# Column sums of two norms and a LayerNorm as pairs of fp32r products with a constant tile

## The chip, the cores and the metric

One core of a Trainium2 chip. The metric is device time in microseconds (us) of one execution; lower is better. PE is TensorE (matmuls; PEld its weight load), DVE is VectorE, ACT ScalarE, POOL GpSimd, SP SyncE, which issues most DMAs. Line numbers with L are those of the kernel before, unless the changed program is named.

## The reference, cut to what matters

One layer of a decoder trunk on 256 prompt rows and 8 × 4 sample rows, all of 2048 channels, in fp32:

```python
h = rmsnorm(x, norm1_g)                                   # x * rsqrt(mean(x^2) + EPS) * g
proj = h @ w_in + b_in                                    # 2048 -> 3072: a, gate, z
u = a * sigmoid(gate)
c = silu(layernorm(depthwise_causal_conv(u_ext, conv_w, conv_b), ln_g, ln_b))
d = multiscale_pool(z_ext, pos0)
p = einsum("btgc,gce->btge", d, pool_w) * pool_scale
x = x + concat([c, p]) @ w_out                            # 2048 -> 2048
h2 = rmsnorm(x, norm2_g)
x = x + square(relu(h2 @ w_ff1)) @ w_ff2                  # 2048 -> 8192 -> 2048
y = rmsnorm(x, norm_f)
```

The outputs are y and the last inputs of the convolution and of the pooling (states).

## The kernel before

**Layout.** All activations are transposed: channels on the 128 partitions, the T = 288 rows of x as columns. xT holds x as 16 tiles of 128 channels. [...]

**Products.** Every large product is done in fp32r with both factors split into a high and a low part, as three matmuls per 128 × 128 weight tile and 288 columns: high·high, low weight·high, high·low activation. Each is one row of L313 in the profile. There are 8,112 of them. `gemm` (L298) makes a group: two banks (256 output channels) times 8 or 16 tiles k of the input. The order of the tiles' parts within a pair of k is fixed; `classes`, a string of 0 and 1, overrides it for the first products of a group (by the parity of tile plus part), and TURN is one such string. `between` names places in a group at which another piece of work is put; the products that follow are issued after its last matmul.

**Weights.** They come by DMA as fp32 (wr, 6 buffers), ACT copies them to fp32r (whi, L263), and the low part (wlo) is made by DVE (L268), POOL (L271) or ACT with a DMA that adds (L265). whi and wlo have 5 buffers each, so each cast on ACT waits until PE is done with a tile five back; which one that is shows in the program's semaphores.

**Stages**, in PE's order: w_in (24 column blocks; conv groups c0 to c7, pool groups p0 to p3 and their own small products P0 to P3), then w_out in two halves of eight groups of 48 products each: first the pool half (input mixp), then, behind LayerNorm and SiLU, the conv half (input mixc). Both halves are added to xT (L554, L575). Then ff1 and ff2 in four chunks, and the final norm.

**The sums.** For a norm `rsqrt_sums` (L219) computes with the squares as weights and a column of ones as moving data: three matmuls (six records, fp32 in two passes each, L228) give the sums as 96 partitions × 3 columns. On these 96 × 3 numbers Sqrt, reciprocal and one correction step run (L234 to L241), and `spread` (L244) multiplies them, broadcast, with the identity (L248, six records) so that each of 128 partitions has the row of 288 factors. The LayerNorm's mean is a product of a matrix of ones with sum_c and with the last c (L525, L526), fp32 in two passes. The placement: the first norm's sums in the first gemm at k = 15 and its rows in the third at k = 2; the LayerNorm by

```python
    BETWEEN = {5: {4: ln_mean}, 6: {6: ln_sums}, 7: {2: ln_rows}}
```

that is, mean in group 5 of the pool half, sums in group 6, rows in group 7. `load_table` (L204) loads ACT's table for the function that comes next. `ln_sums` subtracts the mean from the four c tiles (L531), squares them on ACT (L533), adds on DVE (L537, L538). The rows multiply c into n (L559), SiLU (L562) and a split into mx high (L564) and low (L565) give mixc.

**What sets the order.** Each engine runs its instructions in program order; a scheduler with a simulated timeline makes that order at build time from the code's order, priorities (`later` lowers one) and `issue_after`. So an instruction that waits holds up all that stands behind it on its engine.

## Time and profile before

| | us |
|---|---|
| median of 3 runs | 1090.91 (1090.12 to 1091.37) |
| profiled execution | 1087.89 |
| its span | 1086.1 |
| PE busy | 1071.3 (99%) |
| DVE busy | 632.8 (58%) |
| ACT busy | 476.1 (44%) |
| POOL busy | 181.5 (17%) |
| DMA | 190.71 MB, mean 176 GB/s |

A row of a timeline reads: start, length, engine, line, operation, out<-in, shapes, xcount and, in brackets, the engine's idle time before it and what ended it. A run of like instructions is one row. A matmul's length in a timeline contains its latency (0.29 for one of 288 columns), so successive rows overlap; the pace is seen from start to start. The chain of waits follows the work back from the last instruction; its pieces are listed by start and length.

### The profile page before, as it was taken

The page shows a single profiled execution, that of the slowest core. Times are in us where ns is not written, and L with a number is a line of the kernel's source. Part 1 is how long each engine was busy: PE and PEld are TensorE (multiplying, and loading weights), DVE is VectorE, ACT ScalarE, POOL GpSimd, SP SyncE. Part 2 cuts the span into 40 slices and gives each one's busy share as a digit, 9 for nine tenths or more (in the row PEclk, how much of TensorE's full clock was granted, in tenths as well). Part 3 has the DMA queues.
Part 4 walks back from the last instruction along what each step waited for, and adds up shares of the span by engine and source line. Part 5 has one row for each costly group of instructions (what it writes and reads, how often), then busy time and mean ns, then how long its engine had stood idle before and what let it go on. Part 6 is the DMA issues. An engine that isn't in the chain of part 4 may idle for free.

```text
span 1086.1 us, 19607 instructions
## 1 busy us (share of the span) xinstructions
PE 1071.3 (99%) x8206; PEld 1069.0 (98%) x8206; DVE 632.8 (58%) x812; ACT 476.1 (44%) x584; POOL 181.5 (17%) x212
## 2 busy tenths in 40 slices
PE   8999999999999999999999999999999999999996
PEld 8999999999999999999999999999999999999996
DVE  7899999678555444445454444545544445554553
ACT  8655445475544433334443333444433334444441
POOL 0889989613000000000000000000000000000000
PEclk9999999999999999999999999999999999999998
DMA  9896468545555555555555555555555555555522
GB/s 328 275 278 180 136 174 251 182 152 179 159 171 169 165 171 173 166 167 174 167 167 172 172 164 170 172 169 167 173 168 164 173 173 165 169 172 167 168 76 88
DMA packets 58120, 190.71 MB, mean 176 GB/s; under 512 B 6192, under 2 KB 11312, under 8 KB 58032
## 3 DMA queue, kind: packets, MB, share of 16 engines
q1 hardware_dynamic: 56752, 185.53, 54.4%
q0 software_dynamic: 1008, 3.67, 1.9%
q8 instruction: 64, 1.05, 0.4%
q10 hardware_dynamic: 272, 0.26, 0.1%
q14 instruction: 24, 0.20, 0.0%
HBM read 185.16 MB, written 4.28 MB: 174 GB/s over the span
## 4 chain that ended last, share of the span: by engine, by line
PE 96%; ACT 1%; DVE 1%; issue 1%; DMA 0%; POOL 0%; SPq 0%; DVEq 0%
PE ac L313 95%; PE pp L313 0%; DVE xT L647 0%; ACT whi L263 0%; DMA wr<-in_w 0%; DVE wlo L268 0%; POOL wlo L271 0%; PE idle L231 0%; ACT n L562 0%; PE pt L248 0%; PE pt L228 0%; ACT z_all L384 0%; ACT hx L335 0%; SPq L187 0%; DVE n L559 0%
## 5 line engine op out<-in xcount | busy, mean ns | idle before, releaser
L263 ACT CAST whi<-wr 128x1024 fp32r<-128x1024 f32 (+1 forms) x341 | 354.9, 1041 | 550.5 <-PE ac L313 534.6
L268 DVE TENSOR_TENSOR wlo<-wr,whi 128x1024 fp32r<-128x1024 f32 (+1 forms) x295 | 363.2, 1231 | 353.7 <-ACT whi L263 353.7
L313 PE MATMUL ac<-ax,whi 128*128 128x288 f32 x2048 | 351.5, 292 | 0.0
L313 PE MATMUL ac<-fx,whi 128*128 128x288 f32 x2048 | 350.1, 292 | 0.0
L313 PEld LDWEIGHTS ac<-ax,whi 128*128 128x128 f32 x2048 | 296.2, 187 | 0.0
L313 PEld LDWEIGHTS ac<-fx,whi 128*128 128x128 f32 x2048 | 295.6, 187 | 0.0
L313 PE MATMUL ac<-ax,wlo 128*128 128x288 f32 x1024 | 217.4, 292 | 0.0
L313 PE MATMUL ac<-fx,wlo 128*128 128x288 f32 x1024 | 216.4, 292 | 0.0
L313 PEld LDWEIGHTS ac<-ax,wlo 128*128 128x128 f32 x1024 | 162.6, 187 | 0.0
L313 PEld LDWEIGHTS ac<-fx,wlo 128*128 128x128 f32 x1024 | 162.2, 187 | 0.0
L313 PE MATMUL ac<-hx,whi 128*128 128x288 f32 x768 | 135.3, 293 | 1.7 <-ACT whi L263 1.4
L313 PEld LDWEIGHTS ac<-hx,whi 128*128 128x128 f32 x768 | 112.6, 188 | 2.6 <-ACT whi L263 1.9
L271 POOL TENSOR_TENSOR wlo<-wr,whi 128x512 fp32r<-128x512 f32 x78 | 104.6, 1395 | 32.4 <-ACT whi L263 31.6
L429 DVE SCALAR_TENSOR_TENSOR pc<-u_all,vec,pc 128x256 f32<-128x256 f32 x232 | 99.7, 481 | 2.8 <-ACT pc L426 1.5
L313 PE MATMUL ac<-hx,wlo 128*128 128x288 f32 x384 | 85.2, 293 | 0.2 <-DVE wlo L268 0.2
L313 PEld LDWEIGHTS ac<-hx,wlo 128*128 128x128 f32 x384 | 62.3, 188 | 0.4 <-DVE wlo L268 0.4
L313 PE MATMUL ac<-dx,whi 128*128 128x288 f32 x256 | 46.1, 296 | 0.0
L313 PE MATMUL ac<-mx,whi 128*128 128x288 f32 x256 | 45.1, 294 | 0.1
L612 DVE SCALAR_TENSOR_TENSOR t<-ac,r 128x576 f32<-128x576 f32 x32 | 24.2, 758 | 26.5 <-PE ac L313 25.3
L313 PEld LDWEIGHTS ac<-mx,whi 128*128 128x128 f32 x256 | 37.5, 188 | 0.6 <-ACT mx L564 0.3
L313 PEld LDWEIGHTS ac<-dx,whi 128*128 128x128 f32 x256 | 38.0, 188 | 0.1
L313 PE MATMUL ac<-dx,wlo 128*128 128x288 f32 x128 | 28.6, 297 | 1.4 <-POOL wlo L271 1.4
(107 smaller groups left out, 490.8 us busy)
## 6 DMA issues: line engine op xcount, KB each, us to landing
wr<-in_w SPq DMA_DIRECT2D x335, 512.0 KB, 3.8
wlo<-in_w POOLq DMA_DIRECT2D x7, 512.0 KB, 7.7
xT<-in_xT SPq DMA_DIRECT2D x7, 288.0 KB, 7.9
wr<-in_w SPq DMA_DIRECT2D x5, 256.0 KB, 3.7
out_u_out<-u_all SPq DMA_DIRECT2D x1, 1208.0 KB, 10.7
out_yT<-xT SPq DMA_DIRECT2D x2, 576.0 KB, 2.9
u_all<-in_hist_c SPq DMA_DIRECT2D x8, 136.0 KB, 5.9
out_z_out<-z_all SPq DMA_DIRECT2D x1, 668.0 KB, 8.7
```

The source lines that it names most:

```text
L263: nc.scalar.copy(hi, raw)
L268: nc.vector.tensor_tensor(lo, raw, f32(hi), op=ALU.subtract)
L271: nc.gpsimd.tensor_tensor(lo[:, j : j + 2, :], raw[:, j : j + 2, :], f32(hi[:, j : j + 2, :]), op=ALU.subtract)
L313: last = nc.tensor.matmul(banks[m][:, :T], gets[k // 8](k % 8, m)[w], rhs[k][x], start=j == ends[m][0], stop=j == ends[m][1])
L429: nc.vector.scalar_tensor_tensor(out=dst, in0=up[:, w : w + SEQ], scalar=cwv[:, w : w + 1], in1=pc, op0=ALU.mult, op1=ALU.add)
L612: nc.vector.scalar_tensor_tensor(out=t, in0=bk[:, :, :T], scalar=0.0, in1=both(r2), op0=ALU.max, op1=ALU.mult)
```

## The change

The first norm, the LayerNorm and the second norm no longer use the sums on 96 × 3 and the spread. `parted` splits the 128 × 288 tile to be summed into a high and a low fp32r part (a copy on ACT, a subtraction on DVE or POOL), `column_means` multiplies a constant 128 × 128 tile (1/D or 1/DC in each place) with both parts, so that every partition gets the mean of each column at once, and `inverse_rows` takes Sqrt, reciprocal and the correction step on 128 × 288. The mean of the LayerNorm is done with the same products: sum_c and the last c each in two parts. The final norm keeps the former way. The placement moves: the first norm's products into the third gemm behind 24 of its products, the LayerNorm's mean from k = 4 to k = 6 of group 5, its sum ahead of group 7, the second norm's into ff's first group; TURN moves in the first norm's gemm and from ff's third group to its first. `between` now counts tiles in the order in which they come.

```diff
--- before.py
+++ after.py
@@ -67,6 +67,7 @@
 
+HI = 1
 TURN = "110100" * 4 + "01" * 6 + "1100" * 3
 
@@ -215,6 +216,42 @@
         for t in range(w - 1):
             nc.gpsimd.memset(rcnt[:, w - 2 + t : w - 1 + t], w / (t + 1))
     nc.gpsimd.memset(u_all[:, :, 0:CH], 0.0)
+
+    means = const.tile([P, 2, P], F32R, name="means")
+    nc.vector.tensor_scalar(means[:, 0, :], ones, DC / D, None, op0=ALU.mult)
+    nc.vector.tensor_scalar(means[:, 1, :], ones, 1.0, None, op0=ALU.mult)
+    cst = const.tile([P, 48], F32, name="cst")
+    eps, mean_d = cst[:, 0:1], cst[:, 1:2]
+    nc.vector.memset(eps, EPS)
+    nc.vector.memset(mean_d, 1.0 / D)
+
+    def parted(x, tag, low):
+
+        hl = actp.tile([P, 4, T], F32R, name=nm("hl"), tag="act") if tag == "act" else tmpp.tile([P, 2, T], F32R, name=nm("hl"), tag=tag, bufs=2)
+        nc.scalar.copy(hl[:, HI, :], x)
+        low.tensor_tensor(hl[:, 1 - HI, :], x, f32(hl[:, HI, :]), op=ALU.subtract)
+        return [hl[:, HI, :], hl[:, 1 - HI, :]]
+
+    def column_means(out, w, parts):
+
+        for j, p in enumerate(parts):
+            last = nc.tensor.matmul(out, means[:, w, :], p, start=j == 0, stop=j == len(parts) - 1)
+        return last
+
+    def inverse_rows(name, w, parts, after=None):
+
+        bk, out = ms("mean"), row(name)
+        m, t = bk[:, 0, :T], bk[:, 1, :T]
+        last = column_means(m, w, parts)
+        nc.scalar.activation(t, m, AF.Sqrt, bias=eps)
+        if after is not None:
+            load_table(after, t[:, 0:1])
+        nc.vector.reciprocal(out, t)
+        for scalar, op0, x in ((EPS, ALU.add, m), (-0.5, ALU.mult, m)):
+            nc.vector.scalar_tensor_tensor(out=m, in0=x, scalar=scalar, in1=out, op0=op0, op1=ALU.mult)
+        nc.vector.scalar_tensor_tensor(out=out, in0=m, scalar=1.5, in1=out, op0=ALU.add, op1=ALU.mult)
+        return out, last
 
     def rsqrt_sums(parts, scale, after=None, busy=(0, 0)):
 
@@ -308,7 +345,8 @@
         ahead = None
         for j, (k, m, w, x) in enumerate(todo):
             if j % (len(banks) * len(parts)) == 0:
-                ahead = between[k]() if k in between else None
+                at = step * (j // (len(banks) * len(parts)))
+                ahead = between[at]() if at in between else None
             with tc.issue_after(ahead.ins) if ahead is not None else nullcontext():
                 last = nc.tensor.matmul(banks[m][:, :T], gets[k // 8](k % 8, m)[w], rhs[k][x], start=j == ends[m][0], stop=j == ends[m][1])
         ready.extend(itertools.islice(weights, 1))
@@ -388,10 +426,10 @@
         nc.vector.tensor_tensor(tot[0][:, 0, :], tot[0][:, 0, :], tot[0][:, 1, :], op=ALU.add)
         return [tot[0][:, 0, :]]
 
-    rb = row("rb")
-
+    rows1 = []
 
     cs, pcs = [], []
+    sums = []
     sum_c = tmpp.tile([P, 2, T], F32, name="sum_c", tag="ag2", bufs=2)
 
     def history(i):
@@ -408,7 +446,7 @@
         us = samples(u_all[:, i, UO:UL], US)
         ta, gate = [b[:, :T] for b in banks]
         for b in (gate, ta):
-            nc.vector.tensor_tensor(b, b, rb, op=ALU.mult)
+            nc.vector.tensor_tensor(b, b, rows1[0], op=ALU.mult)
         tg = tmpp.tile([P, 2, T], F32, name=nm("tg"), tag="ag", bufs=2)[:, 0, :]
         nc.scalar.activation(tg, gate, AF.Sigmoid, bias=v("b_in", 8 + i))
         if i == N8 - 1:
@@ -439,6 +477,9 @@
             if i == N8 - 2:
                 for part in (sum_c[:, 1, :], c):
                     nc.gpsimd.tensor_tensor(sum_c[:, 0, :], sum_c[:, 0, :], part, op=ALU.add)
+                sums.extend(parted(sum_c[:, 0, :], "act", nc.gpsimd))
+            if i == N8 - 1:
+                sums.extend(parted(c, "act", nc.vector))
 
     dd = {}
@@ -449,7 +490,7 @@
         gemm(each(bk), hx)
         z = z_all[:, 2 * g : 2 * g + 2, :]
         tz = tmpp.tile([P, 2, T], F32, name=nm("tz"), tag="ag", bufs=2)
-        nc.vector.tensor_tensor(tz, bk[:, :, :T], both(rb), op=ALU.mult)
+        nc.vector.tensor_tensor(tz, bk[:, :, :T], both(rows1[0]), op=ALU.mult)
         for m in range(2):
             b_in = v("b_in", 16 + 2 * g + m)
             nc.scalar.activation(z[:, m, PH:ZO], tz[:, m, 0:SEQ], AF.Identity, bias=b_in)
@@ -487,21 +528,16 @@
 
     for i in range(2):
         history(i)
-    diag = []
     pair0 = each(bank2())
     pair1 = [cvp.tile([P, 512], F32, name=nm("ac"), tag="cv") for m in range(2)]
 
-    def first_sums():
-        diag.append(rsqrt_sums(squares(), 1.0 / D, AF.Sigmoid))
-        return diag[0][2]
-
     def first_rows():
-        pr, last = spread(diag[0])
-        nc.scalar.copy(rb, pr)
+        rb, last = inverse_rows("rb", 0, parted(squares()[0], "ag2", nc.vector), AF.Sigmoid)
+        rows1.append(rb)
         return last
 
-    with tc.issue_after(gemm(pair0 + pair1, hx, between={15: first_sums})):
-        third = conv_products(2, between={2: first_rows}, classes="01" * 18 + TURN)
+    with tc.issue_after(gemm(pair0 + pair1, hx)):
+        third = conv_products(2, between={4: first_rows}, classes="01" * 12 + TURN)
     nc.gpsimd.memset(z_all[:, :, 0:PH], 0.0)
     conv_pair(0, pair0)
     conv_pair(1, pair1)
@@ -522,8 +558,7 @@
 
     def ln_mean():
         norm["mean"] = ms("pmean")[:, 0, :T]
-        nc.tensor.matmul(norm["mean"], ones, sum_c[:, 0, :], start=True, stop=False)
-        return nc.tensor.matmul(norm["mean"], ones, cs[-1][:, 1, :], start=False, stop=True)
+        return column_means(norm["mean"], 1, sums)
 
     def ln_sums():
         ssc = None
@@ -536,14 +571,10 @@
             else:
                 nc.vector.tensor_tensor(ssc, ssc, q, op=ALU.add)
         nc.vector.tensor_tensor(ssc[:, 0, :], ssc[:, 0, :], ssc[:, 1, :], op=ALU.add)
-        norm["sums"] = rsqrt_sums([ssc[:, 0, :]], 1.0 / DC, AF.Silu)
-        return norm["sums"][2]
-
-    def ln_rows():
-        norm["rows"], last = spread(norm["sums"])
+        norm["rows"], last = inverse_rows("rl", 1, parted(ssc[:, 0, :], "act", nc.vector), AF.Silu)
         return last
 
-    BETWEEN = {5: {4: ln_mean}, 6: {6: ln_sums}, 7: {2: ln_rows}}
+    BETWEEN = {5: {6: ln_mean}, 7: {0: ln_sums}}
     behind = nullcontext()
     for g in range(8):
         bk = bank2()
@@ -599,15 +630,20 @@
                 nc.gpsimd.tensor_tensor(ss2, ss2, q2, op=ALU.add)
 
-    r2 = row("r2")
-    ssf = row("ssf")
+    rows2 = []
+
+    def second_rows():
+        rows2.append(None)
+        rows2[0], last = inverse_rows("r2", 0, parted(ss2, "act", nc.vector))
+        return last
+
+    ssf = None
     for ch in range(DFF // FCH):
         fx = []
         for g in range(FCH // 256):
             bk = bank2()
-            gemm(each(bk), x1, classes=TURN if ch == 0 and g == 2 else "")
-            if ch == 0 and g == 0:
-                nc.scalar.copy(r2, rsqrt_rows([ss2], 1.0 / D))
+            gemm(each(bk), x1, between={4: second_rows} if ch == 0 and g == 0 else {}, classes="01" * 12 + TURN if ch == 0 and g == 0 else "")
+            r2 = rows2[0]
             t = tmpp.tile([P, 2, T], F32, name=nm("t"), tag="ag", bufs=2)
             nc.vector.scalar_tensor_tensor(out=t, in0=bk[:, :, :T], scalar=0.0, in1=both(r2), op0=ALU.max, op1=ALU.mult)
             f = tmpp.tile([P, 2, T], F32, name=nm("f"), tag="ag2", bufs=2)
@@ -629,6 +665,7 @@
                 if last:
                     nc.vector.tensor_tensor(xk, xk, banks[m][:, :T], op=ALU.add)
                     if k == 0:
+                        ssf = row("ssf")
                         nc.scalar.activation(ssf, xk, AF.Square)
                     else:
                         qf = tmp("q")
```

The order of instructions changes most at the LayerNorm. (A name ends in two numbers, of the kind and of the tile: whi71 is the 71st cast weight tile; where both programs number tiles alike, whi71 is the same weights.) On ACT, before, from the last square of the LayerNorm on:

```order
L533 ACTIVATE q24_2729<-c4_1733 128x576
L263 COPY whi70_2832<-wr70_2826 128x1024
L235 ACTIVATE st2_2737<-st2_2737 96x3
L204 ACT_TABLE_LOAD
L204 ACTIVATE few_112<-st2_2737 96x1
L263 COPY whi71_2919<-wr71_2915 128x1024
L562 ACTIVATE n1_2837<-n1_2837,vec_85 128x288 x2
L263 COPY whi72_2923<-wr72_2917 128x1024
L562 ACTIVATE n2_2844<-n2_2844,vec_85 128x288 x2
L564 COPY mx1_2841<-n1_2837 128x576
L564 COPY mx2_2848<-n2_2844 128x576
L263 COPY whi73_2990<-wr73_2986 128x1024
```

and in the changed program:

```order
L568 ACTIVATE q24_2767<-c4_1735 128x576
L300 COPY whi71_2927<-wr71_2923 128x1024
L232 COPY hl4_2771<-q21_2756 128x288
L247 ACTIVATE mean2_2774<-mean2_2774,cst_160 128x288
L205 ACT_TABLE_LOAD
L205 ACTIVATE few_112<-mean2_2774 128x1
L300 COPY whi72_2931<-wr72_2925 128x1024
L300 COPY whi73_2998<-wr73_2994 128x1024
L593 ACTIVATE n1_2845<-n1_2845,vec_85 128x288 x2
L593 ACTIVATE n2_2852<-n2_2852,vec_85 128x288 x2
L595 COPY mx1_2849<-n1_2845 128x576
L595 COPY mx2_2856<-n2_2852 128x576
```

The cast whi71 has moved ahead of the LayerNorm's Sqrt and of the copy L232, and whi72 and whi73 ahead of the SiLUs (L562, now L593). By the changed program's semaphores whi71 waits for the last product of group 6 of the pool half, whi72 for the middle of group 7, whi73 for its last product.

On DVE, before, behind the addition of the last squares:

```order
L538 TENSOR_TENSOR q21_2718<-q21_2718 128x288
L268 TENSOR_TENSOR wlo70_2833<-wr70_2826,whi70_2832 128x1024
L234 TENSOR_SCALAR st2_2737<-pt2_2733 96x3
L238 RECIPROCAL st2_2737<-st2_2737 96x3
L239 TENSOR_TENSOR st2_2737<-st2_2737 96x3
L240 TENSOR_SCALAR st2_2737<-st2_2737 96x3
L241 TENSOR_SCALAR st2_2737<-st2_2737 96x3
L554 TENSOR_TENSOR xT_86<-xT_86,ac20_2680 128x576
L268 TENSOR_TENSOR wlo71_2920<-wr71_2915,whi71_2919 128x1024
L559 TENSOR_TENSOR n1_2837<-c1_632,pt2_2733 128x576
```

and in the changed program:

```order
L585 TENSOR_TENSOR xT_86<-xT_86,ac20_2690 128x576
L573 TENSOR_TENSOR q21_2756<-q21_2756 128x288
L305 TENSOR_TENSOR wlo71_2928<-wr71_2923,whi71_2927 128x1024
L233 TENSOR_TENSOR hl4_2771<-q21_2756,hl4_2771 128x288
L250 RECIPROCAL rl1_2775<-mean2_2774 128x288
L252 TENSOR_SCALAR mean2_2774<-mean2_2774,rl1_2775 128x288 x2
L253 TENSOR_SCALAR rl1_2775<-mean2_2774,rl1_2775 128x288
L305 TENSOR_TENSOR wlo72_2932<-wr72_2925,whi72_2931 128x1024
L590 TENSOR_TENSOR n1_2845<-c1_634,rl1_2775 128x576
L590 TENSOR_TENSOR n2_2852<-c2_724,rl1_2775 128x576
```

The addition of group 6 to xT (ac20) and the low part of whi71 now stand ahead of the subtraction L233, the addition also ahead of the sum's last step.

On PE, before, from the sums (L228, 12 products ahead of the end of group 6, bank ac20) to the rows (L248) in group 7 (ac21):

```order
L228 MATMUL pt2_2733<-ones_110,q21_2718 96x1 x3
L313 MATMUL ac20_2680<-dx4_2064,whi65_2669 128x288 x2
L313 MATMUL ac20_2680<-dx4_2064,wlo65_2670 128x288 x2
L313 MATMUL ac20_2680<-dx4_2064,whi65_2669 128x288 x4
L313 MATMUL ac20_2680<-dx4_2064,wlo65_2670 128x288 x2
L313 MATMUL ac20_2680<-dx4_2064,whi65_2669 128x288 x2
L313 MATMUL ac21_2772<-dx1_1257,whi68_2766 128x288 x2
L313 MATMUL ac21_2772<-dx1_1257,wlo68_2767 128x288 x2
L313 MATMUL ac21_2772<-dx1_1257,whi68_2766 128x288 x4
L313 MATMUL ac21_2772<-dx1_1257,wlo68_2767 128x288 x2
L313 MATMUL ac21_2772<-dx1_1257,whi68_2766 128x288 x2
L248 MATMUL pt2_2733<-ident_124,st2_2737 128x96 x3
```

and in the changed program, at the end of group 6:

```order
L351 MATMUL ac20_2690<-dx4_2069,whi65_2679 128x288 x4
L351 MATMUL ac20_2690<-dx4_2069,wlo65_2680 128x288 x2
L351 MATMUL ac20_2690<-dx4_2069,whi65_2679 128x288 x2
L239 MATMUL mean2_2774<-hl4_2771,means_157 128x288 x2
L351 MATMUL ac21_2754<-dx1_1259,whi68_2748 128x288 x2
L351 MATMUL ac21_2754<-dx1_1259,wlo68_2749 128x288 x2
L351 MATMUL ac21_2754<-dx1_1259,whi68_2748 128x288 x4
```

The two products of the LayerNorm's sum stand between groups 6 and 7, and all of group 7 behind them.

## The prediction

> **What bounds the kernel now.** I read the page's chain of waits first, then the windows by stage, then the three engines' timelines around the LayerNorm. The chain's share by engine, and the rows of its pieces (start, length, engine, tile, line):
>
> ```profile
> PE 96%; ACT 1%; DVE 1%; issue 1%; DMA 0%; POOL 0%; SPq 0%; DVEq 0%
> 31.81 0.43 PE pt L228 x6
> 35.52 0.64 PE pt L248 x6
> 199.47 0.48 PE pmean L525 x2
> 202.88 0.48 PE pmean L526 x2
> 220.62 63.43 PE ac L313 x480
> 284.05 0.43 PE pt L228 x6
> 290.17 0.64 PE pt L248 x6
> 290.81 781.06 PE ac L313 x6006
> ```
>
> TensorE is the bound. Its 6,006 products of the last row ran at 781.06/6006 = 130.05 ns each, so a matmul taken out of its queue is a gain in full, and an idle of it a loss in full. The windows say where its time is not 130 ns per product:
>
> ```profile
> 157.00:180.10 23.10, 21.69 (x164) 21.46 (x163) 22.73 (x50) 13.33 (x18) 21.78 (x23) 1.00 0.94 228
> 283.80:322.90 39.10, 39.10 (x302) 39.10 (x302) 20.06 (x23) 18.26 (x21) 0.00 (x0) 1.00 0.52 162
> 322.90:1071.70 748.80, 748.80 (x5762) 748.80 (x5761) 363.26 (x347) 295.81 (x324) 0.00 (x0) 1.00 0.52 163
> ```
>
> (Columns: length; busy time and count of PE, PEld, DVE, ACT, POOL; granted clock; DMA.) The first has 1.4 us without a product, the only stage with a real hole; the last none at all: 748.80/5762 = 129.95 ns. The 2nd norm's stretch has 302 matmuls in 39.10 us, the 12 small ones of L228 and L248 among them: 290 × 0.130 = 37.7, so 1.4 us go to that norm.
>
> **What is taken out.** From the chain's rows: first norm 0.43 + 0.64 = 1.07 us, for which the change has two products (high and low part, 0.26): −0.81. Second norm the same: −0.81. LayerNorm mean: 0.96, for which there are four products (0.52): −0.44. LayerNorm's rows, from PE's timeline at that place:
>
> ```profile
> 211.19 0.59 PE L228 MATMUL pt<-ones,q 128*96 128x1 f32 x6
> 211.65 0.52 PE L313 MATMUL ac<-dx,whi 128*128 128x288 f32 x2
> 213.06 0.70 PE L313 MATMUL ac<-dx,whi 128*128 128x288 f32 x4
> 214.92 0.81 PE L248 MATMUL pt<-ident,st 96*128 96x96 f32 x6
> 215.51 0.51 PE L313 MATMUL ac<-dx,whi 128*128 128x288 f32 x2
> 220.12 0.43 PE L313 MATMUL ac<-dx,whi 128*128 128x288 f32 x2
> 220.62 0.53 PE L313 MATMUL ac<-mx,whi 128*128 128x288 f32 x2
> ```
>
> From start to start: 211.65 − 211.19 = 0.46 and 215.51 − 214.92 = 0.59, together 1.05, against 0.26: −0.79. Sum: **−2.85 us**. There is a little more: the 480 products after the LayerNorm ran at 63.43/480 = 132.1 ns, and 130 comes back only with the sequence TURN (w_out's third group, ff's third). The change puts TURN into ff's first group; between these places lie about 200 products × 2 ns. I take −0.3 (0 to −0.8). So −3.15 if nothing else moved.
>
> **What is added beside PE.** Each sum now needs a copy to fp32r on ACT (L232), a subtraction on DVE or POOL (L233) and, on 288 columns of 128 rows in place of 3 columns of 96, Sqrt, reciprocal and three operations more. The nearest rows:
>
> ```profile
> L411 DVE TENSOR_TENSOR ac<-ac,rb 128x288 f32<-128x288 f32 x16 | 7.0, 457 | 1.5 <-PE ac L313 1.3 <-ACT rb L500 0.2
> L238 DVE RECIPROCAL st<-st 96x3 f32<-96x3 f32 x4 | 0.7, 175 | 1.1 <-ACT st L235 1.1
> L234 DVE TENSOR_SCALAR st<-pt 96x3 f32<-96x3 f32 x4 | 0.6, 154 | 3.3 <-PE pt L228 3.3
> 36.20 0.40 ACT L500 COPY rb<-pt 128x288 f32<-128x288 f32 x1
> 193.30 0.83 POOL L441 TENSOR_TENSOR sum_c<-sum_c,c 128x288 f32<-128x288 f32 x1
> 194.07 12.67 POOL L271 TENSOR_TENSOR wlo<-wr,whi 128x512 fp32r<-128x512 f32 x10
> ```
>
> A copy or Sqrt is 0.40 us, a DVE operation 0.46, one on POOL 0.83. The reciprocal lies between 0.48 (a DVE operation plus the 175 − 154 = 21 ns by which it exceeds one at 3 columns) and 2.5 us (those 21 ns taken per 3 columns: 7 ns × 288 = 2.0, plus 0.46). Where does this lie on PE's path?
>
> First norm: only the rows' use by DVE (L411) waits for it; the products go on as long as they have banks. I take 0 (0 to +0.6, since rb comes 5 to 7 us later than 36.2 + 0.4). Second norm: before, L228 came after ff's first 96 products (284.05); the two products now stand 50 and 65 products into ff, so at about 284.05 − 46 × 0.13 = 278.1 and 280. POOL's last additions to ss2 ended before that, as this row shows, and copy and subtraction fit between: 0.
>
> ```profile
> 273.57 2.00 POOL L599 TENSOR_TENSOR ss<-ss,q 128x288 f32<-128x288 f32 x2 [4.24 <-ACT q L598]
> ```
>
> LayerNorm mean: POOL's subtraction (0.83) stands before its last four lo pieces of 1.27 us; POOL was busy there until 194.07 + 12.67 = 206.7, so it ends at about 206.7 − 5.1 + 0.8 = 202.4. The four products now come together, 12 products (1.6 us) after the place of L526 (202.88). I take 0 (0 to +1). What is left is the LayerNorm's own sum.
>
> **The first new wait, ahead of pool-half group 7.** Before, the sums came in the middle of group 6 and the rows in group 7. Now the two products of L239 stand between group 6's last product and group 7's first, so all of group 7 is queued behind them. And what feeds them is queued, on ACT and on DVE, behind instructions that themselves wait for group 6's last product: on ACT the cast whi71, on DVE group 6's addition to xT (L585, before L554), then the sum's last addition, then the lo part of that cast, then L233. The durations, from DVE's and ACT's timelines:
>
> ```profile
> 209.84 1.05 ACT L263 CAST whi<-wr 128x1024 fp32r<-128x1024 f32 x1 [1.61 <-issue]
> 210.52 0.46 DVE L538 TENSOR_TENSOR q<-q 128x288 f32<-128x288 f32 x1
> 210.93 1.23 DVE L268 TENSOR_TENSOR wlo<-wr,whi 128x1024 fp32r<-128x1024 f32 x1
> 213.52 0.75 DVE L554 TENSOR_TENSOR xT<-xT,ac 128x576 f32<-128x576 f32 x1 [0.28 <-PE ac L313]
> ```
>
> Call Z the moment at which PE would go on to group 7: 213.32 (the third product of the row at 213.06). L554 began at Z + 0.20. DVE: 0.20 + 0.67 + 0.41 (the successor's start is a little before an end) = 1.3, sum there. ACT: cast from 0.2 to 1.2, copy 1.3 to 1.7. DVE: lo part 1.3 to 2.45, subtraction to 2.9, and PE goes on at Z + 3.05. Before it went on at once. **+2.9 us** (2.4 if the queues follow closer, 3.3 with a cast of 1.05 counted in full).
>
> **The second new wait, ahead of the conv half.** Its first product needs mx, that is SiLU of n on ACT and a copy. ACT's order is now: whi72, whi73, four SiLUs, two copies. whi73 waits for group 7's last product. Before, that cast came after the copies. The rows that price it:
>
> ```profile
> 212.47 1.28 ACT L204 ACT_TABLE_LOAD   x1
> 213.88 1.03 ACT L263 CAST whi<-wr 128x1024 fp32r<-128x1024 f32 x1
> 216.09 1.41 DVE L559 TENSOR_TENSOR n<-c,pt 128x576 f32<-128x576 f32 x2
> 217.93 1.03 ACT L263 CAST whi<-wr 128x1024 fp32r<-128x1024 f32 x1
> 218.87 1.14 ACT L562 ACTIVATE n<-n,vec 128x288 f32<-128x288 f32 x2
> 219.91 1.23 ACT L564 CAST mx<-n 128x576 fp32r<-128x576 f32 x2
> ```
>
> Group 7 ends at Z + 3.05 + 0.26 + 48 × 0.133 = Z + 9.7. The cast runs from 9.9 to 10.85. Meanwhile Sqrt, table load and the row operations end at 7.0 or, with the dear reciprocal, 9.0; the lo part of whi72 and the two n (1.41) bring n1 at 9.3 or 10.85, n2 at 10.1 or 11.6. So the reciprocal's price is covered by the cast at both ends. SiLU of n1: 10.85 to 11.9; of n2: to 12.95; copy (0.57): 13.5; PE at 13.6. That is 3.9 us of idle, where before PE stood from 220.12 + 0.26 = 220.38 to 220.62, 0.24. **+3.65 us** (3.3 to 4.4).
>
> **The sum.** −3.15 + 2.9 + 3.65 = +3.4 us. The profiled execution took 1087.89 us (span 1086.1); the median of the three runs shown is 1090.91, 3.0 above it. So the changed kernel's profiled execution should take about 1091.3 and its median **1094.3 us**, slower by 0.3%. Less than 0.2% (2.2 us) can't be told from no change here.
>
> **The rivals.**
>
> *The clock drops in the second wait.* At the kernel's end PE's last matmul ended at about 1075.74, and the clock fell in this window:
>
> ```profile
> 1074.84 0.90 PE L248 MATMUL pt<-ident,st 96*128 96x96 f32 x6
> 1076.00:1080.00 4.00, 0.00 (x0) 0.00 (x0) 4.00 (x5) 0.00 (x0) 0.00 (x0) 0.93 0.55 214
> ```
>
> A mean of 0.93 with half speed at its end means 0.07 × 4.0/0.5 = 0.56 us at half, so it fell at 1079.44, 3.7 us after the last matmul. The second wait, 3.9 us, just passes that. If the clock falls and needs as long to come back, 3.7 us of products run at half speed: +1.85, 1096.1. Against it: one fall shows no threshold to a tenth, and the wait could be 3.5. Chance 0.15.
>
> The Trainium skill ("TensorE: Matmul & The Clock Gate", Part 1: The HAM clock gate) has a free-running window of 3413 ns without work before the gate halves the clock. By that an idle of 3.9 us holds a whole window with a chance of about (3.9 − 3.4)/3.4, an estimate of 0.15, and costs about 1.7 us; the trace agrees so far as its 3.7 us lie between one window and two.
>
> *Not slower: the hole at 157 to 180 closes.* Its row shows 1.4 us without a product, the longest a wait for a lo tile of POOL. The first norm's multiplications come 5 to 7 us later in the changed program and the scheduler has put DVE's and POOL's queues in another order up to there. If the lo tile comes 2 us sooner against PE, the hole is gone, with its slower pace about −2.0: +1.4, 1092.3, within 0.2%. It decides at one wait, L308 of the changed program. Against it: POOL was busy 21.78 of these 23.10 us, and it gets work added. It can grow by as much, too (1096.3). Chances 0.14 and 0.03.
>
> *Faster: the new waits aren't paid.* Were L239 to find its parts ready, for instance because the cast ahead of L232 gets its buffer from group 6's first half, as the cast at 209.84 did (group 6 then had 24 products to go, 3.2 us), the first wait vanishes; then group 7 ends 2.9 us sooner and the second wait stays 3.65 less what n gains. Only with both gone does −3.15 stand: 1087.8. Against it: both casts' places in the order are fixed, and they wait for the last product of groups 6 and 7. Only one gone: −3.15 + 3.65 = +0.5, 1091.4. Chances 0.06 for both gone, 0.05 for one.
>
> *The pace isn't regained.* TURN now ends in ff's first group, with the second norm's products among those that follow. If the pace stays at the 132.1 ns seen after the LayerNorm, some 5,900 products × 2.1 ns = +12: 1106.7. For it: that pace did hold for hundreds of products; against it: after ff's TURN the last window's row has 129.95 for all the rest, and the products of a sum are now of the shape of all others. Chance 0.04.
>
> **How the numbers follow.** Forecast 0.53, clock 0.15, hole closed 0.14 and grown 0.03, one wait 0.05, faster 0.06, pace 0.04. The forecast's own spread (2.4 to 3.3, 3.3 to 4.4, 0 to +1.6 elsewhere, −0.8 to 0) is +2.0 to +5.6. The closed hole takes 2.0 off its low end (0: 1090.9), the clock puts 1.85 on most of its high end (+7.1: 1098.0); for the case of one wait I take the low end down to 1090.2. Outside lie the faster case, the lost pace and the edges: under 0.2. Slower by over 0.2%: 0.53 less 0.03 for its low end, 0.15, 0.03 and 0.04: 0.72. Faster: 0.06. Within 0.2%: 0.03 + 0.14 + 0.05 = 0.22.
>
> **What would show it.** In the changed trace: before group 7's first product a stretch of about 2.9 us without PE, ended by DVE's L233; before the first mx product about 3.9 us, ended by ACT's copy L595, with the cast waiting on PE ahead of the SiLUs; two matmuls of 0.13 us at each sum in place of 12. It is wrong if either stretch is below 1.5 us, if PE waits over 1 us at the first or second norm, if the products after ff's first group aren't at 130 ns, or if the clock's column falls below 1.00 before the end.

## The result and the profile after

| | before | after |
|---|---|---|
| median, us | 1090.51 (4 runs, 1088.02 to 1091.37) | 1126.36 (4 runs, 1124.14 to 1127.46) |
| ratio | | 1.0332 (95%: 1.0315 to 1.035) |
| profiled execution: time, span | 1087.89, 1086.1 | 1127.46, 1125.7 |

Slower by 3.3%, where 0.3% was forecast. From the page of the changed kernel, busy time by engine and the chain by engine:

```profile
PE 1099.9 (98%) x8176; PEld 1097.4 (97%) x8176; DVE 650.3 (58%) x817; ACT 480.7 (43%) x587; POOL 181.3 (16%) x213
PE 96%; DVE 2%; DMA 1%; ACT 1%; SPq 0%; issue 0%; POOL 0%; DVEq 0%; ACTq 0%
```

PE is the bound as before, and is busy for 28.6 us more with 30 fewer matmuls: most of the loss isn't a wait, but products that run slower. The chain of waits (start, length, engine, tile, line) shows where it lies:

```profile
58.09 1.30 POOL prd L471 x2
59.40 8.03 DMA wlo<-in_w
67.47 53.80 PE ac L351 x391
...
205.20 9.52 DVE hl L233
214.77 0.61 PE pmean L239
215.37 10.54 PE ac L351 x60
...
226.61 0.45 DVE q L573
227.06 1.18 DVE wlo L305
228.24 0.38 DVE hl L233
228.66 0.40 PE mean L239
229.06 6.40 PE ac L351 x48
235.48 1.04 ACT whi L300
236.53 2.09 ACT n L593 x4
238.61 0.57 ACT mx L595
239.23 59.60 PE ac L351 x434
298.95 1.99 PE ac L351 x15
301.08 810.39 PE ac L351 x6079
```

The last row is the largest part: 810.39/6079 = 133.31 ns per product, where the row of before (290.81) had 130.05. Above it stand four things new on the chain: an adding DMA for a weight tile in w_in, a subtraction of 9.52 us on DVE ahead of the LayerNorm's mean, and the two waits of the prediction. The windows of the LayerNorm's stretch and of a piece of ff:

```profile
199.30:250.00 50.70, 41.26 (x267) 40.35 (x266) 38.02 (x41) 22.53 (x32) 15.10 (x14) 0.87 0.36 118
330.00:430.00 100.00, 100.00 (x753) 100.00 (x752) 48.60 (x45) 40.40 (x44) 0.00 (x0) 1.00 0.50 164
```

In the first, 9.4 us hold no product and the granted clock was 0.87. In the second PE is never idle and the clock is full, and yet 100 us hold only 750 products, where 130 ns each would give 769 (the count of 753 includes those cut by the edges).

A ledger over all products, from the start records of the traces: the time from the first product of a stage to the first of the next, less 130 ns for each (us):

| stage (products) | before | after | difference |
|---|---|---|---|
| first and third gemm (288) | 4.7 | 5.7 | +1.0 |
| rest of w_in (912) | 1.8 | 7.7 | +5.9 |
| pool half (384) | 3.3 | 14.8 | +11.5 |
| conv half (384) | 0.9 | 3.0 | +2.1 |
| ff, first four groups (384) | 1.6 | 1.2 | −0.4 |
| ff, the rest (5,760) | 0.0 | 19.2 | +19.2 |

The sum, 39.3, is the difference of the two spans (39.6) but for the tail. The second new wait, ahead of the conv half's first product, counts in the pool half. The +1.0 of the first row comes of a half clock at 12.8 us, in the first gemm, which three of the 14 profiles have; without it, the same row is 3.5 to 4.3 us in the eight other profiles with the new first norm, and 4.7 to 5.0 in the three with the old one.

**The pace, product by product.** The records of the changed kernel around ff's first two groups (start in us, whether the moving tile's row of 1,152 bytes is an odd or an even one by its address, ns to the next start, bank):

```
309.987 even 128 ac30        310.508 odd  132 ac31
310.115 odd  132 ac30        310.640 even 132 ac31
310.247 even 128 ac30        310.772 odd  131 ac31
310.375 even 133 ac31        310.903 even 131 ac31
                             311.034 odd  140 ac31
```

Up to 310.247 odd and even rows alternate at 132 and 128 ns: 130.0, reached at 307.3, at the end of TURN. Then comes an even row behind an even one, and from there the gaps soon go 131, 131, 132, 140 over and over: 133.3 ns, to the end of ff, though odd and even rows alternate again. The place is where group 0 (ac30) ends and what is left of group 1 (ac31) begins. For the order of PE there, in the changed program, is: 24 products of group 0, 26 of group 1, one of the sum, 15 of group 1, the other of the sum, 72 of group 0 with TURN, 55 of group 1. The piece of 55 is odd in number and begins with an even row. So the theory to test: PE has two paces, by whether the alternation of odd and even rows is in step or not; TURN brings it into step; any odd slip or short wait behind it takes it out again, and nothing then mends it.

### The profile page after: what moved, and what is told of

Read it like the earlier page. It is cut to its first block, busy times and chain, and to the rows that moved or that the text cites. A ratio compares the mean times of both kernels' runs of the same rounds, so it can differ in the third digit from the quotient of the medians.

```text
span 1125.7 us, 19558 instructions
## 1 busy us (share of the span) xinstructions
PE 1099.9 (98%) x8176; PEld 1097.4 (97%) x8176; DVE 650.3 (58%) x817; ACT 480.7 (43%) x587; POOL 181.3 (16%) x213
## 4 chain that ended last, share of the span: by engine, by line
PE 96%; DVE 2%; DMA 1%; ACT 1%; SPq 0%; issue 0%; POOL 0%; DVEq 0%; ACTq 0%
PE ac L351 95%; DVE hl L233 1%; DMA wlo<-in_w 1%; PE pp L351 1%; DMA xT<-in_xT 0%; DVE xT L684 0%; ACT whi L300 0%; DVE wlo L305 0%; PE idle L268 0%; ACT n L593 0%; POOL prd L471 0%; ACT z_all L422 0%; ACT hx L373 0%; PE mean L239 0%; PE pt L265 0%
## 5 line engine op out<-in xcount | busy, mean ns | idle before, releaser
L351 PE MATMUL ac<-ax,whi 128*128 128x288 f32 x2048 | 357.9, 296 | 0.0
L351 PE MATMUL ac<-fx,whi 128*128 128x288 f32 x2048 | 357.3, 296 | 0.0
L351 PEld LDWEIGHTS ac<-ax,whi 128*128 128x128 f32 x2048 | 301.6, 189 | 0.0
L351 PEld LDWEIGHTS ac<-fx,whi 128*128 128x128 f32 x2048 | 301.4, 189 | 0.0
L351 PE MATMUL ac<-ax,wlo 128*128 128x288 f32 x1024 | 220.9, 296 | 0.0
L351 PE MATMUL ac<-fx,wlo 128*128 128x288 f32 x1024 | 220.1, 296 | 0.0
L351 PE MATMUL ac<-hx,whi 128*128 128x288 f32 x768 | 139.0, 299 | 2.0 <-ACT whi L300 2.0
L351 PEld LDWEIGHTS ac<-hx,whi 128*128 128x128 f32 x768 | 116.7, 192 | 2.6 <-ACT whi L300 2.2
L308 POOL TENSOR_TENSOR wlo<-wr,whi 128x512 fp32r<-128x512 f32 x78 | 103.6, 1390 | 33.4 <-ACT whi L300 32.0
L351 PE MATMUL ac<-hx,wlo 128*128 128x288 f32 x384 | 87.9, 300 | 2.9 <-DMA wlo<-in_w 2.7
L351 PEld LDWEIGHTS ac<-mx,whi 128*128 128x128 f32 x256 | 39.3, 196 | 4.0 <-ACT mx L595 4.0
L678 DVE TENSOR_TENSOR xT<-xT,ac 128x576 f32<-128x576 f32 x24 | 18.1, 753 | 21.3 <-PE ac L351 21.3
```

Source lines behind the costliest of these rows:

```text
L308: nc.gpsimd.tensor_tensor(lo[:, j : j + 2, :], raw[:, j : j + 2, :], f32(hi[:, j : j + 2, :]), op=ALU.subtract)
L351: last = nc.tensor.matmul(banks[m][:, :T], gets[k // 8](k % 8, m)[w], rhs[k][x], start=j == ends[m][0], stop=j == ends[m][1])
L678: nc.vector.tensor_tensor(x2, x2, bk[:, :, :T], op=ALU.add)
```

## The experiments

The edits are to the changed kernel where nothing else is said. Times are compared with runs of the kernel before on the same chip.

### The pace in ff

**e1: TURN in ff's third group again.**

```diff
-gemm(..., between={4: second_rows} if ch == 0 and g == 0 else {}, classes="01" * 12 + TURN if ch == 0 and g == 0 else "")
+gemm(..., between={4: second_rows} if ch == 0 and g == 0 else {}, classes=TURN if ch == 0 and g == 2 else "")
```

> The changed kernel with one edit: TURN stands in ff's third group again, not in its first. Theory (the alternation of odd and even rows is knocked out of step where group 1's held-over products follow group 0's last, and nothing mends it behind that): from ff's fourth group on 130.0 ns per product in place of 133.3, 5,700 products x 3.3 ns = 19 us less, so about 1107 us; the waits at the LayerNorm and in w_in stay. Rival (the pace of 133.3 belongs to something else that the change brought, such as the fp32r sums or the constant tile): 133.3 stays, 1126.

Measured: 1105.79 (ratio 1.0157, 1.0137 to 1.0178). The last row of its chain of waits:

```profile
298.97 790.77 PE ac L351 x6079
```

130.08 ns; ff's rest (5,760 products) lost 0.0 us in place of 19.2. The sums are still products with the constant tile. The rival falls.

**e4: the kernel before without TURN in ff.**

```diff
-            gemm(each(bk), x1, classes=TURN if ch == 0 and g == 2 else "")
+            gemm(each(bk), x1, classes="")
```

> The kernel before with one edit: no TURN in ff's third group. Theory (the pace is a matter of step between the rows' alternation and PE, which the second norm's small matmuls break in the kernel before too): 133.3 ns for ff's rest, 5,700 x 3.3 ns = 19 us more, about 1110 us. Rival (the fp32r sums make the slow pace): 130.0 as before, 1090.5.

Measured: 1109.23 in two executions (ratio 1.0187, 1.0161 to 1.0214), and in its chain of waits:

```profile
291.02 800.80 PE ac L313 x6006
```

133.33 ns, a loss of 19.2 us in ff's rest, to the hundredth that of the changed kernel. So the slow pace is nothing of the new products: the kernel before has it too as soon as nothing brings it back into step.

**e2: group 1 of ff behind group 0, TURN left where the change has it.**

```diff
+            with hold:
-            gemm(...)
+                last = gemm(...)
+            hold = tc.issue_after(last) if ch == 0 and g == 0 else nullcontext()
```

> The changed kernel with one edit: ff's second group is issued only behind the last product of its first, so that none of its products run before it; TURN stays in the first group. Theory (TURN did its work in group 0 and the order of the two groups' pieces undid it): 130.0 ns from ff's first group on, 19 us less, plus a wait of 0 to 2.5 us ahead of the second norm's sums, which now come 24 products into ff without others to go between: 1106 to 1109. Rival (TURN has no effect in that place): 133.3 as in the changed kernel, 1126 or more.

Two executions, 1111.17 and 1131.94 us. The first has a trace: 130.0 ns from TURN in the first group on, and 2.8 us of wait ahead of the sum, which now has no products of group 1 to hide behind, with a half clock behind it; that is 2 us above the range expected. The second is 20.8 us longer, near the 19.2 of the slow pace, but it has no trace: why it is longer stays open.

**e12: as e2, the sum behind 48 products, TURN behind it** (`between={8: second_rows}`, `classes="01" * 24 + TURN`).

> As e2 (second group of ff behind the first, TURN in the first), with the second norm's products behind 48 in place of 24 products and TURN behind these. Theory (in e2 the sum was late at its place, 3.0 us of wait, and TURN mends the step whatever stands behind it as long as no group is cut in two there): no wait at the second norm, 130.0 from the first group on in every execution: 3 us less than e2's profile, as e1 or a little below, 1105. Rival (TURN in the first group is unsure by itself): some executions at 133.3, 20 us longer.

Measured: 1105.79 in 4 runs (1104.56 to 1107.21; ratio 1.0143, 1.013 to 1.0156). Its ff lost 0.35 us in the first four groups and 0.0 behind. So TURN does its work in the first group if products of group 1 don't stand between its pieces. Whether a wait ahead of it, as in e2, makes that unsure is open.

### The wait ahead of the LayerNorm's mean

DVE's and POOL's timelines of the changed kernel:

```profile
204.01 0.48 DVE L467 SCALAR_TENSOR_TENSOR c<-u_all,vec,pc 128x256 f32<-128x256 f32 x1
205.20 9.51 DVE L233 TENSOR_TENSOR hl<-c,hl 128x288 fp32r<-128x288 f32 x1 [0.71 <-ACT hl L232]
```

```profile
203.65 5.04 POOL L308 TENSOR_TENSOR wlo<-wr,whi 128x512 fp32r<-128x512 f32 x4
208.65 0.81 POOL L233 TENSOR_TENSOR hl<-sum_c,hl 128x288 fp32r<-128x288 f32 x1
209.41 4.99 POOL L308 TENSOR_TENSOR wlo<-wr,whi 128x512 fp32r<-128x512 f32 x4
```

A subtraction of 288 columns, 0.45 us where the same L233 runs for the LayerNorm's sum, took 9.51: from 205.20 to 214.71, which is 0.3 us past the end of POOL's row of nine subtractions without a gap (214.40). It began while the second of the nine ran, so it waited for that one and for seven more. The row ahead of it took its normal 0.48 with POOL just as busy; it reads one tile from SBUF and pc from PSUM, L233 two from SBUF.

**e3: another instruction for the subtraction.**

```diff
-        low.tensor_tensor(hl[:, 1 - HI, :], x, f32(hl[:, HI, :]), op=ALU.subtract)
+        low.scalar_tensor_tensor(out=hl[:, 1 - HI, :], in0=x, scalar=1.0, in1=f32(hl[:, HI, :]), op0=ALU.mult, op1=ALU.subtract)   # on DVE
```

> The changed kernel with one edit: the low part that DVE makes of a tile (hl) is a scalar_tensor_tensor (x times 1.0 less the high part) in place of a tensor_tensor; same operands, same place. Theory (DVE's tensor_tensor on two tiles in memory can't start while POOL goes through its queue, and scalar_tensor_tensor can, as the convolution's 0.48 us rows next to a busy POOL show): the 9.5 us of the last c's low part become about 0.5, the 3.6 us of PE ahead of it and the 6 us at half clock behind it (3 us lost) go: about 6.6 us less, 1120. Rival (DVE waited for something else, such as the cast's completion or memory traffic): the row stays at some 9 us and the time at 1126.

Measured: 1126.4 (ratio 1.0345, 1.0329 to 1.036), no gain. Its row on DVE:

```profile
203.17 9.49 DVE L234 SCALAR_TENSOR_TENSOR hl<-c,hl 128x288 fp32r<-128x288 f32 x1 [0.70 <-ACT hl L232]
```

My theory of the kind of instruction fell. What both have in common is two inputs in SBUF, and a row of POOL's to wait for.

**e6: that low part on POOL, TURN as in e1** (`parted(c, "act", nc.gpsimd)`).

> As e1, with the low part of the last c made by POOL in place of DVE. Theory (DVE's subtraction, which reads two tiles in SBUF, is shut out while POOL's subtractions follow each other without a gap; the other kind of instruction of e3 read the same two tiles): no DVE instruction stands there, the part costs POOL 0.8 us, PE's 3.6 us wait and the 3 us lost at half clock behind it go: about 6.5 us less than e1, 1099. Rival (the last c itself is late): the wait stays, 1105.

Measured: 1100.24 (ratio 1.0097, 1.0074 to 1.012); its profiled execution is 5.9 us shorter than e1's, but only 3.8 of that lie in the pool half (9.7 us lost in place of 13.5), in place of the 6.5 expected. The half clock did not go: it came behind the first new wait instead (at 220.0 us, where e1 has it at 215.5, behind the mean's). Another 1.9 us lie in w_in, which e6 leaves as it is, and whose rest lost 7.0 to 9.6 us in the seven profiles with this first norm. POOL did the part in its row, and PE's four products came without a wait:

```profile
207.42 0.80 POOL L233 TENSOR_TENSOR hl<-c,hl 128x288 fp32r<-128x288 f32 x1
```

```profile
209.09 0.53 PE pmean L239 x4
```

So the last c wasn't late: DVE was shut out while POOL worked. The Trainium skill ("SBUF — State Buffer", SBUF: two separate sides) says that VectorE and GpSimd share a port pair, which a VectorE operation with two SBUF inputs takes or waits for as a whole; these runs agree that one waits for the other. But they don't make a rule of the 9.5 us. DVE and POOL in the changed kernel's trace, 30 us ahead of that row:

```profile
174.74 1.67 DVE L514 TENSOR_TENSOR dx<-d,dx 128x576 fp32r<-128x576 f32 x1
```

```profile
173.22 6.85 POOL L308 TENSOR_TENSOR wlo<-wr,whi 128x512 fp32r<-128x512 f32 x5
```

This subtraction, too, reads two tiles in SBUF and met a row of L308 without a gap, and it came in behind the one instruction of POOL that was running; POOL's next took 1.85 us in place of 1.3. Why the one at 205.20, in the same way in all six traces that have it there, waited for the end of POOL's row isn't shown.

**e5: the LayerNorm as before, both norms changed, TURN as in e1.**

```diff
-        return column_means(norm["mean"], 1, sums)
+        nc.tensor.matmul(norm["mean"], ones, sum_c[:, 0, :], start=True, stop=False)
+        return nc.tensor.matmul(norm["mean"], ones, cs[-1][:, 1, :], start=False, stop=True)
...
-        norm["rows"], last = inverse_rows("rl", 1, parted(ssc[:, 0, :], "act", nc.vector), AF.Silu)
+        norm["sums"] = rsqrt_sums([ssc[:, 0, :]], 1.0 / DC, AF.Silu)
...
-    BETWEEN = {5: {6: ln_mean}, 7: {0: ln_sums}}
+    BETWEEN = {5: {4: ln_mean}, 6: {6: ln_sums}, 7: {2: ln_rows}}
```

> The changed kernel with TURN in ff's third group (e1) and the LayerNorm's mean, sum and rows as they were before; the two norms stay changed. Theory (of what is left after e1, the LayerNorm's three new waits and the half clock behind two of them are the larger part): e1's losses over 130 ns per product of 13.5 us in the pool half and 2.0 in the conv half fall back to the 3.3 and 0.9 of before: 11 us less than e1, about 1094.5. Rival (the waits come from the later work of w_in and would arise with the old LayerNorm too): less than 4 us gained, 1102 or more.

Measured: 1094.24 (ratio 1.0035, 1.0018 to 1.0053). Pool half 3.29 and conv half 0.88 us lost, as before the change. All of the LayerNorm's loss is thus the new way of doing it in this place, 11.4 us of what e1 loses in these two halves.

### The first norm

DVE's timeline of the changed kernel:

```profile
41.76 1.96 DVE L250 RECIPROCAL rb<-mean 128x288 f32<-128x288 f32 x1 [6.09 <-ACT few L205]
43.76 0.97 DVE L252 SCALAR_TENSOR_TENSOR mean<-mean,rb 128x288 f32<-128x288 f32 x2
44.76 0.46 DVE L253 SCALAR_TENSOR_TENSOR rb<-mean,rb 128x288 f32<-128x288 f32 x1
```

The factors are ready at 45.2, against 36.20 + 0.40 = 36.6 before. PE then stood for 0.27 us at the head of c3 (47.9), where a bank wasn't free; the step, which TURN had restored at 45.1, was lost there, and w_in went on at 133.3. And POOL's products for the convolution (prd) came late, and behind them the adding DMA of the chain's row at 59.40, for which PE waited 2.9 us. In the kernel before this DMA was issued at 56.06 and landed 6.0 us later, 0.9 us ahead of PE's use.

**e7: the first norm's products at the head of the third gemm, TURN as in e1** (`between={0: first_rows}`).

> As e1, with the first norm's two products at the head of the third gemm, 24 products (3.1 us) sooner. Theory (the factors rb come too late: at 45.2 in place of 36.6 us; so the bank of c3 isn't free, 0.3 us, which breaks the step and costs 870 products x 3.3 ns = 2.9 us, and POOL issues the adding DMA of a weight tile late, behind its products for the convolution: 3.0 to 3.8 us of wait and 1.6 at half clock): rb comes some 3 us sooner, the bank wait and the slow pace go (3 us less), the wait for the DMA shrinks by up to 3 us and with it the half clock: 3 to 8 us less than e1, 1098 to 1103. Rival (POOL's order alone makes the DMA late): only the pace comes back, 1102 to 1103, or nothing.

Measured: 1101.44 (ratio 1.0114, 1.0092 to 1.0136). The rest of w_in lost 4.4 in place of e1's 9.5 us: the wait for the DMA fell from 3.6 to 0.6 us and the half clock behind it went, as the theory had it. (PE waited although the DMA was issued at 53.72, sooner than before the change: it took 9.5 us.) c3's bank was free, but another wait of 0.37 us, for the adding DMA of c3's second weight tile, broke the step at 49.4, so the pace did not come back: that part missed.

**e8: the kernel before with the second norm alone changed, TURN in ff's third group.**

> The kernel before with the second norm alone done as in the changed kernel, TURN in ff's third group. Theory (the products themselves are worth what they take out of PE's queue): its 12 small matmuls (1.07 us) become two of 0.13; loss in ff's first four groups 0.8 in place of 1.6 us: 0.8 us less than before, 0.1%, at the edge of what 5 rounds can tell. Rival (the sums cost more than they save wherever they stand): same or slower.

Measured: 1087.16 in 12 runs against 1089.57; ratio 0.9986 (0.9975 to 0.9998). Loss in ff's first four groups: 0.56 in place of 1.58 us. This is the part of the change that pays, and the one version here that is ahead of the kernel before, by 0.14% (0.02 to 0.25).

**e9, e10, e11: both norms changed, the old LayerNorm.** e9 has the first norm's products behind 180 products, where the sums of before stood, with the table load kept out of the reciprocal's way; e10 has them behind 192; e11 is e9 with the table load as in the change.

```diff
-    with tc.issue_after(gemm(pair0 + pair1, hx)):
-        third = conv_products(2, between={4: first_rows}, classes="01" * 12 + TURN)
+    with tc.issue_after(gemm(pair0 + pair1, hx, between={15: first_rows})):   # e9, e11
+        third = conv_products(2, classes="01" * 18 + TURN)
...
-            load_table(after, t[:, 0:1])
+            with tc.issue_after(sq.ins):                                       # e9, e10; sq is the Sqrt
+                load_table(after, cst[:, 0:1])
```

> The kernel before (old LayerNorm) with both norms done by products: the second as in e8, the first at the end of the first gemm (behind 180 products, where the sums stood before), and ACT's table load reads a constant, so that the reciprocal doesn't stand behind it. Theory (the late factors were what cost w_in, not the products): rb is ready by 37 to 38 us as before, c3's bank is free, the pace is 130.0 from the third gemm on, no wait for the adding DMA; 0.8 us less than e8: 1086.4, 0.3% below before. Rival (the first norm's work on 288 columns disturbs DVE and POOL wherever it stands): a wait over 1 us in w_in or a pace of 133.3, 1089 to 1095.

> As e9, with the first norm's products at the head of the third gemm (behind 192 products). Theory: rb is about 1.6 us later than in e9 and still ahead of c3's bank: the same time as e9 within 0.5 us. Rival (there is no slack in w_in): a wait as in e7, 0.4 us or more, which breaks the step: 3 us more than e9.

> As e9, but the table load reads the square root's result as in the changed kernel, so that the reciprocal waits for it. Theory (1.3 to 1.5 us of the late rb are this wait): rb 1.4 us later than in e9; no wait of PE if the slack is that large, the same time as e9 within 0.5 us; if c3's bank is late even so, 3 us more.

Measured: 1092.22 (ratio 1.0021, 1.0011 to 1.003), 1094.03 (1.0036, 1.0023 to 1.0049) and 1093.06 (1.0019, 1.0009 to 1.0029). My expectation of 1086.4 missed; the rival's time was right. e10 is 1.8 us above e9, between its theory (the same) and its rival (3 us more). e11's table load did hold the reciprocal up, by 1.5 us, but rb came at 38.9, no later than e9's, and the times are alike. The executions of each differ by 3 to 5.5 us; the profiled one is e9's slowest, but the fastest of e10 and of e11. The rows of e9 on DVE and on POOL, and POOL's of before:

```profile
34.19 1.96 DVE L251 RECIPROCAL rb<-mean 128x288 f32<-128x288 f32 x1 [1.92 <-ACT mean L247]
36.64 1.23 DVE L306 TENSOR_TENSOR wlo<-wr,whi 128x1024 fp32r<-128x1024 f32 x1 [0.50 <-ACT whi L301]
37.78 0.96 DVE L253 SCALAR_TENSOR_TENSOR mean<-mean,rb 128x288 f32<-128x288 f32 x2
38.78 0.46 DVE L254 SCALAR_TENSOR_TENSOR rb<-mean,rb 128x288 f32<-128x288 f32 x1
```

```profile
58.05 0.78 POOL L304 DMA_DIRECT2D wlo<-in_w  x1
```

```profile
56.06 1.12 POOL L266 DMA_DIRECT2D wlo<-in_w  x1
```

Even from the old place rb comes at 39.2, 2.6 us late: the reciprocal costs 1.96 us, the row operations 1.4, and between them DVE waits for a cast and makes a weight tile's low part, 1.6 us. POOL issues the DMA 2.0 us later than before; it landed 8.3 us on, and PE waited 2.8 us (1.8 in e11, 2.7 in e10) and then ran at 133.3 until w_out. There was no such slack in w_in. The lateness of rb alone does not decide: in e10 the DMA was issued at 56.23, nearly as before, and still came 2.7 us late, because it took 8.6 us. This DMA landed in 5.7 to 6.0 us in the three traces with the old first norm (before, e4, e8), and in 7.3 to 9.5 us in the eleven with the new one. Why it takes longer there isn't shown.

## Why the prediction was wrong

**What is taken out** (−2.85): right in kind, two records of 0.13 us at each sum; in size shown for the second norm alone, which gave −1.0 (e8), for 0.81 of matmuls and a little pace. The LayerNorm's part can't be told from its waits.

**The first new wait** (2.9): 2.79 ahead of the sum's two products (1.84 and 0.95), which stand between the last product of group 6 and the first of group 7. The chain's rows at 226.61 to 228.66 are the queue that was named: group 6's addition, the sum, the cast's low part, L233.

**The second new wait** (3.9): 3.94 beyond a product's 0.13. The rows at 235.48 to 238.61 are the cast, the SiLUs and the copy. The reciprocal at 1.96 us lay inside its bounds and was covered.

**The clock** (a rival with 0.15): it came true, three times over. The clock fell behind the second wait, behind the mean's and behind the DMA's in w_in, for 6.8, 6.8 and 3.4 us. Products came every 240 ns there, so an estimate from these numbers is a cost of about 7 us, against the 1.85 that one fall was priced at. The rival's condition, an idle of 3.7 us, was not what decides: two of the three waits were shorter (2.9 and 3.45); see the last section.

**LayerNorm mean, "I take 0 (0 to +1)"**: wrong, 3.45 us of wait and a half clock behind it. The step costed the four products by POOL's part alone. The low part of the last c on DVE, 0.46 us by the rows, was not looked at next to POOL's row of ten subtractions, which the prediction had itself quoted (194.07 12.67). It wasn't the size of a term but one that was left out: DVE's wait for POOL.

**First norm, "I take 0 (0 to +0.6)"**: rb came 8.6 us later, not 5 to 7. The bank's wait, 0.27, lay inside the bounds; what it sets off, the slow pace, did not, and POOL's adding DMA was not looked at. With its wait of 2.9 us and the half clock, the rest of w_in lost 5.9 us more.

**The pace** is the step that failed, and the largest. "The change puts TURN into ff's first group ... I take −0.3 (0 to −0.8)" took it that TURN works wherever it stands, and the rival "the pace isn't regained" got a chance of 0.04 and 2.1 ns per product. It was 3.33 ns over 5,760 products, 19.2 us, half of the loss. The 132.1 ns behind the 2.1 were no pace of their own: in the start records of the kernel before, the conv half runs at about 133 ahead of its TURN and at 130.0 behind it. What decided could have been read from the order: the prediction counted that the sum's products stand 50 and 65 products into ff, which is only so since products of group 1 stand between those of group 0; so what is left of group 1 follows TURN, and an odd number of it.

**The hole at 157 to 180** closed in the changed kernel's profile, as its rival had it: the same product that waited 1.58 us before (166.02) waits 0.20 (173.10). It gave 1.4 us, within the 5.9 of w_in, and did not matter.

## What to carry to other kernels

Where a loop runs at a pace that depends on a pattern (here odd and even rows), a change's price isn't its own instructions but whether the pattern still holds behind it; look at the order behind the last place that restores it. A chain made longer on an idle engine is free only up to its slack, so measure the slack to the next user first, the ones two steps on too. And move one thing at a time: of this change one part in three paid, 0.14%, and it pays by itself.

## What the runs showed of the hardware

**Two paces at a full clock.** 130.0 or 133.3 ns for the same products, no wait, clock 1.00; the same loss of 19.20 us in ff in the changed kernel, in e3 and in e4. What in the chip has the two beats isn't shown.

**The half clock.** The granted clock in windows of the changed kernel around two of its falls and in its first new wait (226.00), and of e6 in its first new wait (217.20), in its second and behind it:

```profile
64.40:67.50 3.10, 0.36 (x4) 0.12 (x2) 3.10 (x10) 2.10 (x2) 3.10 (x6) 0.98 1.05 247
70.00:71.00 1.00, 1.00 (x6) 1.00 (x6) 1.00 (x4) 0.00 (x0) 0.00 (x0) 0.61 1.03 336
226.00:228.50 2.50, 0.40 (x1) 0.19 (x1) 2.50 (x4) 1.41 (x2) 0.00 (x0) 1.00 0.69 210
235.40:239.20 3.80, 0.04 (x1) 0.00 (x0) 3.41 (x5) 3.72 (x7) 0.00 (x0) 0.85 0.41 138
243.00:246.00 3.00, 3.00 (x18) 3.00 (x18) 1.43 (x2) 1.72 (x4) 0.00 (x0) 0.69 0.01 3
```

```profile
217.20:220.20 3.00, 0.61 (x3) 0.19 (x1) 2.98 (x5) 1.48 (x2) 0.00 (x0) 0.96 0.74 251
228.20:232.00 3.80, 0.23 (x2) 0.00 (x0) 2.57 (x4) 3.54 (x6) 0.00 (x0) 1.00 0.47 149
232.20:234.20 2.00, 1.99 (x13) 2.00 (x14) 2.00 (x4) 0.53 (x1) 0.00 (x0) 0.86 0.72 231
```

Worked out as in the prediction, the clock of the changed kernel fell at 67.38 and came back at 70.78 (3.4 us), and fell at 238.06 and came back at 244.86 (6.8 us). The second fall came 2.6 us after the end of the last product (235.15 + 0.29), sooner than the 3.7 us of the kernel's end. The length of a wait alone doesn't decide. The first new wait (some 1.9 and 0.9 us, with one product between) left the clock at 1.00 in the changed kernel and dropped it in e6, at 219.96. The second, 3.9 us in both, dropped it within the wait in the changed kernel, and in e6 only at 233.64, 1.4 us after PE had gone on.

The place of the wait in a fixed beat does decide. By each trace's clock records all changes of the clock within it lie a whole number of 3.413 us apart: from 67.38 to 238.06 are 50 of these, from 70.78 to 244.86 are 51. All 14 traces, from 5 to 1060 us, have 4,275 pieces of this beat that begin at a full clock. The 27 of them with 2.10 us or more without a product (130 ns counted for each) end in a fall; the 4,248 with 1.99 us or less don't. The free-running window of 3413 ns that the Trainium skill describes ("TensorE: Matmul & The Clock Gate", Part 1: The HAM clock gate) agrees with the pieces, and with a fall that depends on where in a window the wait lies. A window without any work, as the prediction took it from there, is not needed: 2.10 of its 3.41 us were enough.

**A reciprocal of 288 columns** takes 1.96 us on DVE, four times another operation of that size (0.46).
